# One hybrid encoder layer on one core: the mixers' due times paced by stage, the last block's cut moved from column 18 to 20, a stream of weight sums started later

## The chip, the cores and the metric

One core of a Trainium2 chip runs the whole program in one launch. The metric is device time in microseconds (us); three runs of the kernel before are at hand, and one profiled execution.

## The reference, cut to what matters

One layer over two streams of 1024-wide tokens: a prompt of 2048 behind 16 meta tokens, and 64 new sample tokens with their own states. A norm, one wide projection, three mixers that are causal scans over time, an output projection, and a SwiGLU block:

```python
def _trunk(x, states, segs, p):
    ...
        m, ns = _mixer(_rmsnorm(x, p['norm1_w'][l]), l, *st, segs, p)
        x = x + m
        x = x + _swiglu(_rmsnorm(x, p['norm2_w'][l]), p['w_gate'][l], p['w_up'][l], p['w_down'][l])
    ...
    return _rmsnorm(x, p['final_norm_w']), [jnp.stack(lst) for lst in new]

def _mixer(h, l, ssm0, conv0, rw0, shift0, hg0, segs, p):
    proj = jnp.einsum('btd,dn->btn', h, p['w_in'][l])
    z, xbc, dt_raw, rw_in, hg_in = _split(proj, [SSD_INNER, SSD_CONV_DIM, SSD_HEADS, RW_IN, HG_IN])
    ...   # y_ssd: chunked state-space scan; y_rw: RWKV-7 scan; y_hg: gated linear recurrence
    y = jnp.concatenate([y_ssd, y_rw, y_hg], axis=-1).astype(h.dtype)
    out = jnp.einsum('btm,md->btd', y, p['w_out'][l])

def _swiglu(h, wg, wu, wd):
    return (jax.nn.silu(h @ wg) * (h @ wu)) @ wd
```

Everything is float32. The hidden width of the SwiGLU block is 2816, which the kernel cuts into 22 columns of 128.

## The kernel before, in words

**Tokens and tiles.** The tokens stand in 17 tiles of 128 (tile 0 holds the 64 sample tokens and the 16 meta tokens). Each float32 product is done as three matmuls on parts `hi` and `lo`. A weight is split into its parts on first use (`load_unit`: a 256 KB load into the ring `raw`, ACT for `hi`, POOL or DVE for `lo`), stored to memory, and from the second use on loaded as a 512 KB pair into the ring `w` (5 buffers; `raw` has 3).

**Stages of the weight products.** The projection runs over three groups of tiles. Then come three early blocks of three tiles each (`EARLY`, class `Ffn`): `out` (the output projection, residual, norm, transposes), `ffn` (the 22 columns, two at a time, called a pair here: gate and up products, then `down` of the pair before), `rest` (the last down and the final norm). Block 0 uses the weights of `out` and `ffn` for the first time and so splits them; blocks 1 and 2 load the pairs. The eight last tiles (`LATE`) follow in another scheme (`tokens_first`, `columns`) that multiplies sums of weight quarters; `t_sums` forms these sums (loads into `raw`, four subtractions or additions on DVE, stores) and `prep_sums` does so for twelve of them ahead of time.

**The mixers** work beside the weight products, one tile after the other: stream `rw` (`rw_mixer`, `rw_tail`) and stream `hs` (`hg_mixer` and `ss_mixer` in step). Their small matmuls write the banks `c`, `h` and `po`, while the weight products write `g`. Much of a mixer is DVE and ACT work, and each goes through memory several times (`rin`, `hin`, `sin` loads; `psc` and `psx` of the small triangular solver). The outputs `y` are stored tile by tile and loaded again by `out`, for the late tiles into `ya`.

**The placing.** The order in which instructions are written comes from a clock in the code, `now`. Every weight product yields its cost in full-speed microseconds of TensorE (columns / 2360), and `flow` adds it to `now` and steps each stream that is due. A step yields its distance to the next one, and `Stream.step` sets the due time: `self.t = max(self.t, now[0] - 1.0) + d * self.scale`. The scales are 1.08 for rw, 1.03 for hs; an hs tile is 13 steps of 6.0. `drain` steps the streams until the outputs asked for are written, with no weight product between. This order is a priority: the framework builds each engine's queue from it by a simulated clock, and may set an instruction that is ready ahead of an earlier one that is not.

**Where the last block is cut.** `early()` writes block 2's columns up to `SWITCH` as a part of `flow`, then `drain(ALLY(range(NT)))` writes what is left of the mixers, their memory is given up, the 24 loads of `ya` and the remaining columns of block 2 follow. `prep_sums` is a stream like the mixers, appended after block 1's `out`.

Of the kernel before, what the change touches and what calls it, by code (L numbers as in the profile page):

```python
# [23 lines left out]
NFF = DFF // P  # L24
# [15 lines left out]
GLO = 3  # L40
URB = 6
RWX, HSX, HSD = 1.08, 1.03, 6.0
COL = 1 / 2360
AHEAD = 4
KOUT = [8, 9, 10, 11, 0, 1, 2, 3, 4, 5, 6, 7]
# [1 line left out]
DSTEP = (-1, 2, 6, 9)  # L47
FW = 3
NH = 4
SWITCH = 18  # L50
PRE = 3
TAIL = 4
CW = 384
# [25 lines left out]
def body(tc, A, O, blocks=None, supers=None, dbg=None):  # L79
# [7 lines left out]
    def pool(st, name, bufs=1, **kw):  # L87
        return st.enter_context(tc.tile_pool(name=name, bufs=bufs, **kw))
# [20 lines left out]
    def mm(out, lhsT, rhs, start, stop, more=False):  # L109

        return T.matmul(out, lhsT, rhs, start=start, stop=stop, skip_group_check=more)  # L111
# [145 lines left out]
    def gemm_cm(w, hTs):  # L257

        banks = [gbank() for _ in hTs]
        for k0 in range(0, KD, 4):  # L260
            hi, lo = load_unit(w[:, k0 * P:(k0 + 4) * P])
            for ps, ((hhi, hlo), n) in zip(banks, hTs):
                for k in range(k0, k0 + 4):
# [3 lines left out]
                    mm(ps[:, :n], wl, hhi[:, k, :n], False, k == KD - 1)  # L267
                yield 12 * n * COL
        return banks

    def gemm_tm(w, hT, tiles):

        banks = [gbank() for _ in tiles]
        for k in range(KD):
            wh, wl = load_unit(w[k * P:(k + 1) * P, :])
            for ps, (o, n) in zip(banks, tiles):
# [3 lines left out]
                mm(ps[:n], l, wh, False, k == KD - 1)  # L280
            yield 3 * len(tiles) * 512 * COL
        return banks

    def gemm_dt(w, hTs):
# [8 lines left out]
        for ps, ((hhi, hlo), n) in zip(banks, hTs):  # L293
            for k in range(KD):
                mm(ps[:16, :n], wt[:, k], hhi[:, k, :n], k == 0, False)
                mm(ps[:16, :n], wt[:, k], hlo[:, k, :n], False, k == KD - 1)
            yield 16 * n * COL
        return banks
# [686 lines left out]

    streams, done = [], set()
    ready = {"rw": [], "hs": []}
    now = [0.0]

    class Stream:  # L990
        def __init__(self, gen, scale):
# [2 lines left out]
        def step(self):  # L994
            d = next(self.gen, None)
            if d is None:
                self.live = False
            else:
                self.t = max(self.t, now[0] - 1.0) + d * self.scale

    def mixers(kind, fn):
        for t in range(last_tile + 1):
# [15 lines left out]
    def flow(gen):  # L1018

        for cost in gen:  # L1020
            now[0] += cost
            for s in list(streams):
                while s.live and s.t <= now[0]:
                    s.step()
            streams[:] = [s for s in streams if s.live]

    def drain(keys):
        while not all(k in done for k in keys):
            for s in list(streams):
                s.step()  # L1030
            streams[:] = [s for s in streams if s.live]
# [113 lines left out]
    class Ffn:  # L1145
# [31 lines left out]
        def out(self):  # L1177
# [10 lines left out]
            def scaled(i):  # L1188
                hs[i] = self.w2k(), self.w2k()
                rms_scaled(fp, acc[:, i, :], self.lens[i], nw, hs[i])  # L1190
# [5 lines left out]
            def mms(i, k, wh, wl):  # L1196
                yh, yl = (ya[0][:, k], ya[1][:, k]) if k < 8 else (y3[0][:, k - 8], y3[1][:, k - 8])
                ti = slice(i * P, i * P + P)
                mm(banks[i], yh[:, ti], wh, k == KOUT[0], False)
                mm(banks[i], yh[:, ti], wl, False, False)  # L1200
                mm(banks[i], yl[:, ti], wh, False, k == KOUT[-1])

            for half_ in range(2):
                cs = slice(half_ * 512, half_ * 512 + 512)
                banks = [gbank() for _ in tiles]
                for k in KOUT[:8] if half_ else KOUT:
                    w = load_unit(A["w_out"][half_, k])
                    for i in range(self.nt):
                        mms(i, k, *w)
                    yield 3 * self.nt * 512 * COL  # L1210
                if half_ == 0:
# [4 lines left out]
            for i in range(self.nt):  # L1216
# [3 lines left out]
                if i < 2:  # L1220
                    scaled(i)
                yield 12 * 512 * COL
            hi, lo = self.hT = self.hl(self.fp, "h2", KD)
# [25 lines left out]
        def rest(self):  # L1249
# [4 lines left out]
            for i in range(self.nt):  # L1254
                for hf in range(2):
                    self.down_tile(i, hf, mhi, mlo, wds[hf])
                    yield 3 * CF * 512 * COL
                self.final(i, fw)
# [25 lines left out]
    if supers:  # L1284
# [4 lines left out]
        def early():  # L1289
            drain(ALLY(EARLY[0]))  # L1290
            fs[0].start()
            for i, f in enumerate(fs):
                drain(ALLY(EARLY[i]))
                yield from f.out()
                if i == 1:
                    streams.append(Stream(prep_sums(), 1.0))
                if i + 1 < len(fs):
                    yield from f.ffn(0, NFF - AHEAD)
                    drain(ALLY(EARLY[i + 1]))
                    fs[i + 1].start()  # L1300
                    yield from f.ffn(NFF - AHEAD, NFF)
                    yield from f.rest()
                else:
                    yield from f.ffn(0, SWITCH)

# [9 lines left out]
        def t_sums(key, q, queue):  # L1315

            def ld(n):
                r = mk(ring, [P, 512], tag="raw", bufs=RB)
                queue.dma_start(r, q[n])
                return r  # L1320

            def st(n, r):
                d = tdram[key, n] = dram.tile([P, 512], F32, tag=f"{key}{n}", name=f"{key}{n}")
                G.dma_start(d, r)

            a, b = ld(3), ld(1)
            V.tensor_tensor(a, a, b, SUB)
            st("t3", a)
            c_ = ld(0)
            V.tensor_tensor(b, b, c_, SUB)  # L1330
            st("t1", b)
            V.tensor_tensor(c_, a, c_, ADD)
            st("t2", c_)
            d_ = ld(2)
            V.tensor_tensor(d_, d_, c_, SUB)
            st("t4", d_)

        def quarters(key, kk):
            if key in ("w_gate", "w_up"):
                return [A[key][2 * kk + f][:, h * 512:h * 512 + 512] for h in range(2) for f in range(2)]  # L1340
            if key == "wo":
                k = kk // 2 * 4 + kk % 2
                return [A["w_out"][d, k + 2 * h] for h in range(2) for d in range(2)]
            return [A["w_down"][(2 * kk + h) * P:(2 * kk + h + 1) * P, d * 512:d * 512 + 512] for h in range(2) for d in range(2)]

        def prep_sums():
            for key, kks in (("wo", (4, 5, 0, 1, 2, 3)), ("w_gate", range(PRE)), ("w_up", range(PRE))):
                for kk in kks:
                    t_sums(f"{key}{kk}", quarters(key, kk), nc.sync)
                    yield 35.0  # L1350

        def parts(raw):
            wt = mk(ring, [P, 2, 512], F32, tag="w", bufs=WB)
# [73 lines left out]
        xs2 = [[dram.tile([P, D], F32, tag=f"xs{h}{j}", name=f"xs{h}{j}") for j in range(NH)] for h in range(2)]  # L1427

        flow(early())
        drain(ALLY(range(NT)))  # L1430
        stA.close()
# [10 lines left out]
        lq = pool(st, "lq", side="right", reuse_waits="tile")  # L1442
        flow(fs[-1].ffn(SWITCH, NFF))
        flow(fs[-1].rest())
# [354 lines left out]
```

## Time and profile before

| | |
|---|---|
| three runs | 3514.22, 3523.47, 3526.61 us (median 3523.47) |
| profiled execution | 3511.97 us, span 3510.2 us |
| mean granted TensorE clock | 0.982 |
| busy: PE, PEld, DVE, ACT, POOL | 3366.0, 2942.8, 2212.6, 1226.9, 778.5 us |
| DMA | 860.42 MB, mean 245 GB/s |

The stages can be told apart in the timeline of TensorE by the tiles that its matmuls read:

| stage | from, to (us) |
|---|---|
| projection, with mixers | 0 to 1357 |
| block 0: out, columns | 1357 to 1476, to 1856 |
| block 1: out, columns | 1856 to 1950, to 2318 |
| block 2: out, columns | 2318 to 2397, to 2730 |
| late tiles | 2730 to 3510 |

How to read it: the span is that of one execution; engines overlap, and a stage's length is set by whichever wait ends last in it. PE and PEld are the two halves of TensorE (matmul and weight load). A clock of 1.00 is TensorE's full speed. DMA share is the busy share of the core's 16 DMA engines. In a table by stage, each engine's column is its busy time with the number of instructions in brackets.

### The profile page before, as it was taken

The numbers are of one execution on the slowest core, as the hardware profiler recorded it, in microseconds if no ns is written. First come the engines' busy times: TensorE is split into PE (matmuls) and PEld (weight loads), VectorE is DVE, ScalarE is ACT, GpSimd is POOL, SyncE is SP. The second block draws the span as 40 slices with busy tenths as digits, with TensorE's granted clock in tenths as the row PEclk, the third lists the DMA queues.
The fourth block names the chain that finished last, engine by engine and source line by source line (L and its number), as shares of the span: only waits on it lengthen the run. The fifth ranks groups of instructions, "written<-read, shape, count | busy, mean of one in ns | idle before, by whom it ended". The sixth has DMA issues, their size and how long they took to land.

```text
span 3510.2 us, 61013 instructions
## 1 busy us (share of the span) xinstructions
PE 3366.0 (96%) x22588; PEld 2942.8 (84%) x22588; DVE 2212.6 (63%) x4961; ACT 1226.9 (35%) x2635; POOL 778.5 (22%) x1122
## 2 busy tenths in 40 slices
PE   7999999999999998899898999999999999999998
PEld 7999789999799996787787888888988887888786
DVE  3358555567665677687877767667643676665453
ACT  4445233344343443343452212223210352233342
POOL 3324201102112112344442211111100123431101
PEclk9999999999999998899999999999999999999999
DMA  9776875565775667889889898686788567875856
GB/s 321 233 227 209 298 237 160 172 180 163 247 223 173 193 194 245 288 305 315 293 303 346 297 328 275 227 285 203 224 259 267 199 209 263 304 273 165 295 191 215
DMA packets 427123, 860.42 MB, mean 245 GB/s; under 512 B 112432, under 2 KB 212280, under 8 KB 424776
## 3 DMA queue, kind: packets, MB, share of 16 engines
q1 hardware_dynamic: 394376, 749.01, 64.9%
q0 software_dynamic: 32448, 107.50, 8.4%
q8 instruction: 178, 2.92, 0.3%
q14 instruction: 121, 0.99, 0.1%
HBM read 603.81 MB, written 252.54 MB: 244 GB/s over the span
## 4 chain that ended last, share of the span: by engine, by line
PE 69%; DMA 11%; DVE 10%; issue 4%; ACT 2%; POOL 2%; SPq 2%; POOLq 0%; DVEq 0%; ACTq 0%
PE g L111 47%; PE d L111 11%; PE c L111 5%; PE h L111 4%; DMA w<-w 3%; DMA raw<-in_w_up 1%; DMA hin<-hg 1%; POOL w L222 1%; DMA hg<-stage 1%; DVE tp L640 1%; DVE Xp L641 1%; DMA raw<-in_w_gate 1%; PE po L111 1%; DVE acc L1278 1%; DVE gcv L418 1%
## 5 line engine op out<-in xcount | busy, mean ns | idle before, releaser
L111 PE MATMUL g<-hhi,w 128*128 128x384 f32 (+3 forms) x3312 | 831.7, 330 | 10.1 <-POOL w L222 3.7
L111 PEld LDWEIGHTS g<-hhi,w 128*128 128x128 f32 (+1 forms) x3312 | 580.0, 188 | 23.9 <-POOL w L222 4.5
L111 PE MATMUL g<-h2hi,w 128*128 128x384 f32 (+1 forms) x2112 | 548.6, 335 | 21.9 <-DMA w<-w 7.9
L111 PE MATMUL g<-hlo,w 128*128 128x384 f32 (+3 forms) x1680 | 550.5, 328 | 0.0
L111 PEld LDWEIGHTS g<-h2hi,w 128*128 128x128 f32 x2112 | 376.4, 190 | 35.2 <-ACT w L220 8.6
L111 PE MATMUL g<-h2lo,w 128*128 128x384 f32 (+1 forms) x1056 | 349.6, 331 | 0.0
L111 PEld LDWEIGHTS g<-hlo,w 128*128 128x128 f32 (+1 forms) x1680 | 314.1, 187 | 6.2
L222 POOL TENSOR_TENSOR w<-raw,w 128x512 fp32r<-128x512 f32 x180 | 244.0, 1358 | 338.3 <-ACT w L220 276.3
L111 PE MATMUL g<-w,mhi 128*128 128x512 f32 x792 | 259.3, 404 | 8.3 <-DMA w<-w 3.5
L220 ACT ACTIVATE w<-raw 128x512 fp32r<-128x512 f32 x240 | 150.1, 628 | 194.2 <-PE g L111 50.0
L111 PEld LDWEIGHTS g<-h2lo,w 128*128 128x128 f32 x1056 | 200.3, 190 | 2.8
L111 PE MATMUL g<-w,hhi 128*128 128x512 f32 (+1 forms) x544 | 178.1, 407 | 7.4 <-DMA w<-w 4.2
L111 PEld LDWEIGHTS g<-w,mhi 128*128 128x128 f32 x792 | 145.0, 189 | 43.6 <-DVE acc L1278 4.5
L640 DVE TENSOR_TENSOR tp<-Xp,b4k 128x60 f32<-128x60 f32 (+24 forms) x527 | 125.1, 237 | 52.0 <-DMA b4k<-psc 38.9
L1278 DVE TENSOR_TENSOR acc<-g,acc 128x512 f32<-128x512 f32 (+1 forms) x198 | 132.1, 682 | 39.2 <-PE g L111 38.9
L111 PE MATMUL g<-w,mlo 128*128 128x512 f32 x396 | 155.7, 394 | 0.0
L111 PE MATMUL g<-w,op 128*128 128x512 f32 x600 | 142.8, 395 | 0.0
L111 PEld LDWEIGHTS g<-w,op 128*128 128x128 f32 x600 | 112.3, 187 | 27.3
L641 DVE TENSOR_TENSOR Xp<-Xp,tp 128x60 f32<-128x60 f32 (+24 forms) x527 | 122.9, 233 | 13.3
L230 POOL TENSOR_TENSOR rs<-ss,half 128x1 f32<-128x1 f32 (+2 forms) x51 | 34.6, 681 | 424.6 <-DVE ss L228 261.0
L111 PEld LDWEIGHTS g<-w,hhi 128*128 128x128 f32 (+1 forms) x544 | 99.5, 189 | 32.4 <-DMA w<-w 6.5
L356 DVE SCALAR_TENSOR_TENSOR stage<-graw,cvec,stage 128x384 f32<-128x384 f32 (+2 forms) x98 | 53.5, 549 | 113.5 <-ACT graw L351 34.4
(449 smaller groups left out, 6619.2 us busy)
## 6 DMA issues: line engine op xcount, KB each, us to landing
w<-w SPq DMA_DIRECT2D x893, 512.0 KB, 4.4
hin<-hg SPq DMA_DIRECT2D x16, 1280.0 KB, 7.7
rin<-rw SPq DMA_DIRECT2D x16, 896.0 KB, 6.2
raw<-in_w_gate SPq DMA_DIRECT2D x56, 256.0 KB, 4.4
raw<-in_w_up SPq DMA_DIRECT2D x56, 256.0 KB, 4.3
hg<-stage SPq DMA_DIRECT2D x64, 192.0 KB, 2.5
raw<-in_w_out SPq DMA_DIRECT2D x48, 256.0 KB, 4.4
sin<-ss SPq DMA_DIRECT2D x16, 768.0 KB, 4.9
```

What stands on the lines that cost most here:

```text
L111: return T.matmul(out, lhsT, rhs, start=start, stop=stop, skip_group_check=more)
L220: S.activation(hi, raw, AF.Copy)
L222: (G if units[0] % 4 < GLO else V).tensor_tensor(lo, raw, wt[:, 0], SUB)
L230: G.tensor_tensor(rs[:n], ss[:n], half[:n, 0:w], ALU.pow)
L356: V.scalar_tensor_tensor(st[:, a0:a1], raw[:, s0:s0 + a1 - a0], mu, st[:, a0:a1], MUL, ADD)
L418: V.scalar_tensor_tensor(cvt[:, :M], raw[:, j:j + M], tap(j), cvt[:, :M], MUL, ADD)
L640: V.tensor_tensor(tv, _bc(Xp[:, 0:m, q], 2, w), _bc(Up[:, q, q + 1:32], 1, m), MUL)
L641: V.tensor_tensor(Xp[:, 0:m, q + 1:32], Xp[:, 0:m, q + 1:32], tv, ADD)
L1278: V.tensor_tensor(self.acc[:n, i, cs], ps[:n], self.acc[:n, i, cs], ADD)
```

## The change

A factor `pace` multiplies the distance between the steps of every stream (mixers and sums alike). It is 1.0 through the projection, 1.36 from block 0's `out` on, 1.02 from block 1's on. Block 2 is cut at column 20 in place of 18. The stream of the sums is appended after ten columns of block 1 in place of none, and its steps are 32 apart in place of 35 (times the pace).

```diff
+PACE = (1.36, 1.02, 1.02)
...
-SWITCH = 18
+SWITCH = 20
+AFTER = 10
...
-    now = [0.0]
+    now, pace = [0.0], [1.0]
...
-                self.t = max(self.t, now[0] - 1.0) + d * self.scale
+                self.t = max(self.t, now[0] - 1.0) + d * self.scale * pace[0]
...
                 drain(ALLY(EARLY[i]))
+                pace[0] = PACE[i]
                 yield from f.out()
-                if i == 1:
-                    streams.append(Stream(prep_sums(), 1.0))
                 if i + 1 < len(fs):
-                    yield from f.ffn(0, NFF - AHEAD)
+                    if i == 1:
+                        yield from f.ffn(0, AFTER)
+                        streams.append(Stream(prep_sums(), 1.0))
+                    yield from f.ffn(AFTER if i == 1 else 0, NFF - AHEAD)
                     drain(ALLY(EARLY[i + 1]))
...
                     t_sums(f"{key}{kk}", quarters(key, kk), nc.sync)
-                    yield 35.0
+                    yield 32.0
```

## The prediction

> **What bounds the kernel now.** I read the page first (slices, then the matmul rows), then a table of busy time by stage with cuts at the borders of the stages, then the same table for the tile `g` alone (all weight products write a bank of that name), and last the waits of TensorE inside the stages that the change touches.
>
> ```profile
> span 3510.2 us, 61013 instructions
> PE   7999999999999998899898999999999999999998
> PEclk9999999999999998899999999999999999999999
> DMA  9776875565775667889889898686788567875856
> ```
>
> TensorE is busy in nearly every slice; the dull ones are 15 to 20, which is where the first early block runs. The stages in one table (out and feed-forward of block 0, of block 1, then block 2 in four pieces: out, columns with mixers beside them, columns without, the last 59 us):
>
> ```profile
> core 0: us, PE busy (x) PEld busy (x) DVE busy (x) ACT busy (x) POOL busy (x), PEclk, DMA share, GB/s
> 1357.00:1476.00 119.00, 96.09 (x655) 74.67 (x654) 86.86 (x186) 50.34 (x109) 36.96 (x33) 0.80 0.82 276
> 1476.00:1856.00 380.00, 352.55 (x2641) 306.01 (x2642) 297.14 (x610) 166.67 (x359) 166.30 (x133) 0.97 0.88 305
> 1856.00:1950.00 94.00, 81.15 (x586) 64.28 (x585) 64.84 (x176) 24.71 (x68) 21.13 (x31) 0.92 0.90 324
> 1950.00:2318.00 368.00, 361.58 (x2611) 323.45 (x2611) 261.53 (x633) 91.83 (x211) 56.50 (x71) 1.00 0.83 280
> 2318.00:2397.00 79.00, 73.84 (x629) 59.18 (x628) 49.21 (x138) 22.27 (x63) 12.41 (x19) 0.99 0.78 269
> 2397.00:2604.00 207.00, 206.77 (x1478) 189.87 (x1477) 121.03 (x301) 43.78 (x109) 23.29 (x23) 0.99 0.70 223
> 2604.00:2671.00 67.00, 57.40 (x285) 51.05 (x284) 27.34 (x36) 7.01 (x11) 0.00 (x0) 0.97 0.96 298
> 2671.00:2730.00 59.00, 59.00 (x306) 54.38 (x305) 20.47 (x34) 7.47 (x18) 0.82 (x2) 1.00 0.74 241
> ```
>
> Block 0 (1357 to 1856) leaves TensorE idle for 23 + 27 us, block 1 for 13 + 6, block 2 for 5 + 0 + 10 + 0. Block 0 is the only one that also splits weights (POOL 166 us in its columns against 57 in block 1's). The matmuls of `g` alone, and for the whole run those of the three banks that only mixers write:
>
> ```profile
> 1357.00:1476.00 119.00, 63.30 (x243) 44.45 (x242) 8.49 (x16) 4.54 (x10) 0.80 0.82 276
> 1476.00:1856.00 380.00, 284.25 (x1477) 233.83 (x1478) 63.63 (x110) 9.47 (x22) 0.97 0.88 305
> 1950.00:2318.00 368.00, 301.97 (x1478) 257.85 (x1479) 68.55 (x111) 11.42 (x23) 1.00 0.83 280
> 2397.00:2604.00 207.00, 176.77 (x885) 155.06 (x886) 38.73 (x62) 6.84 (x14) 0.99 0.70 223
> ...
> 0.00:3511.00 3511.00, 300.78 (x4556) 233.64 (x4556) 264.00 (x471) 201.64 (x455) 41.61 (x77) 0.98 0.74 245
> ...
> 0.00:3511.00 3511.00, 274.77 (x2792) 221.92 (x2792) 173.68 (x359) 26.79 (x51) 0.98 0.74 245
> ...
> 0.00:3511.00 3511.00, 35.66 (x816) 34.00 (x816) 10.11 (x17) 0.98 0.74 245
> ```
>
> The last three rows give the size of a mixer tile: (4556 + 2792 + 816) / 17 = 480 matmuls for one tile of both streams. All matmuls of a stage less those of `g` are mixers: 1164, or 2.42 tiles, in block 0's columns; 1133, 2.36 tiles, in block 1's; 593, 1.24 tiles, in block 2's; 412, 0.86 tiles, in block 0's out.
>
> **What a tile costs where it stands now.** The products have their cost in the code, in units of the placing clock: a block's out is 49.9 units, block 0's columns 229.2 (320 tokens), block 1's 257.7 (384 tokens), a pair of columns 15.6 and its down products 7.8. The last 59 us hold two pairs and three downs, 54.7 units, and no mixer: 1.08 us a unit. By that, block 0's columns would take 247 us alone, so 133 us went with 2.42 tiles: 55 us a tile. Block 1: 368 − 278 = 90 for 2.36, 38 a tile. Block 2, 2397 to 2604: the 885 products are about seven pairs and six downs less a little, 155.5 units or 168 us, so 39 for 1.24, 32 a tile. The same work costs 55 us beside block 0 and 32 us beside block 2. That difference is what the change can collect.
>
> **Pace of block 0: 1.36.** No instruction is added or removed; due times move, and with them the order on every queue (TensorE, DVE, ACT, POOL, and SP with `rin`, `hin`, `sin`, the solver's `psc`/`psx` trips). I followed the placing rule of `flow` and `Stream.step` through the yields with both sets of constants. At the end of block 0 the hs stream stands at tile 10.83 before and 10.00 after, the rw stream at 12.51 and 11.81. So 0.83 hs tiles and 0.70 rw tiles leave block 0: 0.77 tiles, 0.14 of them from its out, 0.63 from its columns. At the block's own price the columns give back 0.63 × 55 = 35 us. The out stage is mostly a hand-over, so I price its share at block 1's 38: 5 us. Sum −40.
>
> What is late next in block 0:
>
> ```profile
> PE g L111 <- ACT w L220: 8.0, 5, 3.3
> PE h L111 <- ACT us L920: 4.4, 2, 2.3
> PE g L111 <- POOL w L222: 3.6, 7, 0.9
> PE g L111 <- DVE w L222: 2.5, 4, 1.0
> ```
>
> These are TensorE's longest waits in 1476 to 1856. The products' own waits (rows of `g`) are for split weights, 14 us, and the rest for mixer steps that came due too soon. Fewer mixers shorten the second kind, not surely the first: a weight takes 256 KB in and 512 KB out whatever stands beside it. DMA had 0.88 × 380 = 334 us of work there. A mixer tile brings at least two large loads:
>
> ```profile
> hin<-hg SPq DMA_DIRECT2D x16, 1280.0 KB, 7.7
> rin<-rw SPq DMA_DIRECT2D x16, 896.0 KB, 6.2
> ```
>
> 2.2 MB, at 305 GB/s 7 us, so 4.5 us for 0.63 tiles. The fullest stretch in the table is 0.96, and (334 − 4.5) / 0.96 = 343 us: the columns can shrink by 37 us before DMA is the floor, and my 35 lies just inside. For that reason I take nothing for the 1.8 tiles that stay in block 0 becoming cheaper (they could: 1.8 × (55 − 38) = 30, of which the floor lets 2 through).
>
> **Pace of blocks 1 and 2: 1.02, and SWITCH 18 to 20.** Columns 18 and 19 and one more down join the stretch with mixers, 23.4 units. In block 1 the count of mixers stays (3.62 hs tiles before, 3.68 after). In block 2 the last hs step was due in pair 6 of the columns, 59 units ahead of the final drain; after, it comes due with the last down before the drain, and one step is left to it. So 0.77 tiles go beside pairs 7 to 9, at the price of block 2: 0.77 × 32 = +24. Bounds: 29 at block 1's price, and 14 if they fill the 9.6 idle us of 2604 to 2671. That idle time I leave in, because its cause moves along:
>
> ```profile
> PE g L111 <- DMA w<-w: 8.9, 6, 2.4
> ...
> 2602.13 0.55 POOL L883 DMA_DIRECT2D y<-hin  x1 [3.99 <-DVE hin L882]
> ...
> L1441 SPq DMA_DIRECT2D ya<-y x24: 518/630/1752, 2605.1 to 2633.4; - x24
> ```
>
> The 24 loads of `ya` start 3 us after the last mixer output and fill DMA (0.96) for some 30 us, and TensorE waits for weights meanwhile. After the change they start at the end of pair 9's downs, with pair 10 and two downs to run: 31 units, 34 us, and 43 with the same waits. The next stage needs the first third of `ya` at its start and the last third 11 us later, so 30 us fit, with little left. I take 0 here; the other bound is a lag of the chain as long as 20 us.
>
> **Sums later** (after column 10 of block 1, 32 apart in place of 35).
>
> ```profile
> L1319 SPq DMA_DIRECT2D raw<-in_w_out x24: 328/333/792, 1846.1 to 1998.2; - x24
> ...
> L1319 SPq DMA_DIRECT2D raw<-in_w_up x12: 328/333/1117, 2066.1 to 2123.6; - x12
> ```
>
> By the placing clock they were due from the start of block 1's columns (1950) to block 2's third down. They ran from 1846 to 2124, as soon as block 0's last weight had left the `raw` ring: independent work is pulled ahead of its place. I expect that again, so the later place moves them little: 0. If they do move, out 1 is rid of them, where TensorE waited for loaded weights in this row (1856 to 1950), and that is the bound below:
>
> ```profile
> PE g L111 <- DMA w<-w: 6.5, 4, 3.6
> ```
>
> Against it 5 us at most, were the 12 sums (48 DVE subtractions and 25 MB) to run beside `ya` instead.
>
> **Sum.** −35 − 5 + 24 + 0 + 0 = −16 us. The profiled execution took 3511.97 us (span 3510.2), 11.5 below the median of the runs, 3523.47. So 3496 for an execution like the profiled one, and 3507.5 as a median. A difference of 0.3%, 10.6 us, is about what a measurement of this kernel can tell from no change.
>
> **Rivals.**
> 1. Block 0 is held by its weights, and the mixers only fill the holes. Then its columns don't shrink by 55 a tile but by little more than block 2 charges. For it: 14 us of waits for split weights and DMA at 0.88. Against it: TensorE was busy 352 of 380 us and DMA has room up to 0.96. With 38 a tile: −24 − 5 + 24 = −5; with 32, 0; with a floor some us higher, +5: 3518 to 3528. Chance 0.28.
> 2. The end of block 2 turns into a wait, and the kernel gets slower. Place: the border to the last tokens at 2730. The last mixer output lands late, `ya` behind it, and the weights of pair 10 interleave with 6 MB on a full DMA. It decides from a lag of about 16 us beyond the 34 to 43 us of cover. For it: both streams have round trips through memory, and no step of theirs is left to trail behind in slack. Against it: TensorE waited 0.2 us for mixers between 2397 and 2604, so they keep up there. Worth +8 to +25: 3531 to 3549. Chance 0.16.
> 3. The hand-over from out to columns in block 0 closes, since fewer mixer steps stand on DVE ahead of the norm. That stage took 119 us against 79 in block 2, with DVE at 87 and 49 us busy. Half of that difference would bring 20 us more: 3479 to 3497. Against it: the stage's first 25 us are a wait for the previous stage's buffers, where the pace isn't set yet. Chance 0.08.
> The granted clock goes with the third: 0.80 in that stage, 0.99 in the same stage of block 2. The Trainium skill, TensorE: Matmul & The Clock Gate, section "Part 1: The HAM clock gate", has it that about 3.4 us without matmul work halves the clock until a busy window has passed; the trace agrees in that 0.80 goes with 23 idle us of 119. By that rule 119 × 0.2 = 24 us are the most that steady work could win back there, an estimate, and it would put the time at the third rival's.
> That the sums stay where they ran is my own forecast; it changes no case.
>
> **How the numbers follow.** My forecast, −5 to −25 around −16, 3498 to 3518: 0.48. Rival 1: 0.28, rival 2: 0.16, rival 3: 0.08. Faster by over 0.3% (below 3513): three quarters of the forecast, 0.36, rival 3, 0.08, and a small part of rival 1 where the columns do shrink, 0.06: 0.50. Slower (above 3534): 0.15 from rival 2 and 0.02 from a high rival 1: 0.17. Same: 0.33. The likeliest case alone spans 3498 to 3518. The range goes from rival 3's middle, 3487, to the lower part of rival 2, 3533; outside stay half of rival 3 and most of rival 2, under 0.2.
>
> **What would show it.** Right: block 0's columns near 345 us in place of 380, with about 860 mixer matmuls in them in place of 1164; block 1's columns within 8 us of 368; 2604 to 2671 filled with mixers, the last `y<-hin` some 25 to 35 us before the last columns' end; the raw loads of the sums still starting near block 0's end. Wrong: DMA at 0.93 or more in block 0 with `g` waiting for split weights over 25 us (rival 1); a wait of the first products after block 2 for `ya` or `op` (rival 2); block 0's out under 105 us (rival 3). The forecast falls if the price of a mixer tile beside block 0 doesn't come from its density there.

## The result, and the profile after

The changed kernel took 3563.91 us (median of 4 runs, 3559.21 to 3567.03) against 3522.72 for the kernel before on the same chip: a ratio of 1.0116, interval 1.0099 to 1.0133. That is 41 us slower. The prediction had 3507.5, with a chance of 0.17 for slower; its range ended at 3533.

The page after, its span and TensorE's row of slices:

```profile
span 3562.8 us, 60980 instructions
...
PE   7999999999999998899888999999998999999998
```

TensorE has a new dull slice, the 31st (2672 to 2761): the end of block 2. The stages with cuts at the borders of this execution: out and columns of block 0, of block 1, then block 2 as out, columns up to the last pair, and the last pair to the border.

```profile
core 0: us, PE busy (x) PEld busy (x) DVE busy (x) ACT busy (x) POOL busy (x), PEclk, DMA share, GB/s
1359.70:1476.50 116.80, 94.05 (x646) 73.45 (x645) 83.71 (x184) 49.28 (x106) 36.51 (x32) 0.81 0.80 278
1476.50:1864.90 388.40, 357.39 (x2615) 303.32 (x2614) 285.28 (x604) 158.90 (x345) 169.41 (x129) 0.97 0.87 302
1864.90:1953.70 88.80, 77.61 (x447) 61.88 (x443) 62.91 (x146) 30.12 (x76) 20.23 (x31) 0.94 0.92 322
1953.70:2304.40 350.70, 342.29 (x2310) 306.29 (x2310) 222.33 (x543) 71.27 (x162) 43.53 (x60) 0.99 0.82 278
2304.40:2401.80 97.40, 84.80 (x659) 66.21 (x658) 51.09 (x118) 28.31 (x74) 15.55 (x22) 0.92 0.66 233
2401.80:2721.20 319.40, 315.42 (x2331) 285.49 (x2329) 190.12 (x483) 63.11 (x153) 29.08 (x30) 0.99 0.70 222
2721.20:2778.10 56.90, 37.37 (x183) 33.39 (x183) 24.37 (x33) 11.34 (x29) 2.96 (x4) 0.82 0.84 249
```

Block 0's columns are 388 us, not 345. They still hold 2615 matmuls, and the rows of `g` alone have 1468 of them, so 1147 are mixers where the prediction had 860. Block 1's columns, where it expected no change, are 17 us shorter; out 2 is 18 us longer; block 2's columns (the last two rows) are 44 us longer.

The stages of both kernels, with the mixer matmuls m that start in each (counted record by record). In columns 0 this gives 1188 and 1162, where differences of rows give 1164 and 1147: a view of the tile `g` also holds eight matmuls of each rw tile that read a tile of that name.

| | out 0 | columns 0 | out 1 | columns 1 | out 2 | columns 2 | rest of the span |
|---|---|---|---|---|---|---|---|
| before, us | 118.4 | 379.9 | 94.3 | 367.6 | 79.7 | 331.9 | 2138.3 |
| before, m | 412 | 1188 | 346 | 1156 | 390 | 606 | |
| change, us | −1.7 | +8.5 | −5.5 | −16.9 | +17.6 | +44.4 | +6.1 |
| change, m | −8 | −26 | −144 | −298 | +26 | +450 | |

The sum is +52.6. The medians differ by 41: the profiled execution of before was 11.5 us below its median. The projection, where the change does nothing, took between 1352 and 1367 us in the profiled executions; columns 0 took 378.9 to 384.3 us in five of them that hold the same 1188 mixer matmuls (before, e2, e3, e11, e12). So differences of a few us in one stage are not read. The table says it in one line: one tile (476 matmuls) left blocks 0 and 1, mostly block 1, for 16 us, and came to block 2 for 62.

**Where the tiles went.** The outputs of the hs stream in time, after and then before (start, duration, instruction, and in brackets POOL's idle time before it):

```profile
1723.83 0.62 POOL L885 DMA_DIRECT2D y<-hin  x1 [1.45 <-DVE hin L884]
1812.95 0.59 POOL L885 DMA_DIRECT2D y<-hin  x1 [0.74 <-DVE hin L884]
1935.71 0.59 POOL L885 DMA_DIRECT2D y<-hin  x1 [8.90 <-DVE Xp L643]
2234.80 0.62 POOL L885 DMA_DIRECT2D y<-hin  x1 [10.42 <-DVE hin L884]
...
2731.95 0.55 POOL L885 DMA_DIRECT2D y<-hin  x1 [3.82 <-DVE hin L884]
```

```profile
1719.90 0.61 POOL L883 DMA_DIRECT2D y<-hin  x1 [1.25 <-DVE Xp L641]
1848.44 0.61 POOL L883 DMA_DIRECT2D y<-hin  x1 [3.84 <-DVE hin L882]
1933.33 0.54 POOL L883 DMA_DIRECT2D y<-hin  x1 [4.07 <-DVE hin L882]
2130.15 0.54 POOL L883 DMA_DIRECT2D y<-hin  x1 [1.13 <-DVE hin L882]
```

The stream that was to be held back by 36% wrote its eleventh tile at 1812.95, 35 us earlier than before. By its due times that tile was to begin only at the start of out 1. One tile later comes a gap of 299 us (1935.71 to 2234.80), where before had an output at 2130, and the last output moves from 2602 to 2732. The rw stream did slow down: its twelfth output moves from 1802.68 to 1875.88. A tile of rw has 316 matmuls, one of hs 164. In the first ten pairs of block 0's columns hs rose from 2.20 to 2.71 tiles and rw fell from 2.18 to 1.36, 176 matmuls fewer in all; those ten pairs took 331.4 us before and 332.3 after. The last pair, with the two downs behind it, took 150 of them back: 240 rw matmuls ran there in place of 44, and it is 7.7 us longer (before, then after):

```profile
1807.30:1855.80 48.50, 44.70 (x308) 37.04 (x306) 43.40 (x64) 29.97 (x70) 18.31 (x15) 1.00 0.84 291
```

```profile
1808.70:1864.90 56.20, 51.13 (x457) 40.76 (x456) 39.66 (x84) 22.34 (x49) 23.09 (x18) 0.94 0.92 325
```

In the whole of columns 0 rw falls from 734 to 670 matmuls and hs rises from 454 to 492.

**The end.** TensorE's waits in the last 57 us of block 2, and the loads behind them:

```profile
PE g L113 <- DVE ya L1471: 19.5, 1, 19.5
```

```profile
L1445 SPq DMA_DIRECT2D ya<-y x24: 594/832/1039, 2736.9 to 2756.3; - x24
```

One single wait of 19.5 us, from 2743.5 to 2763.1. The row names DVE's work on `ya`, but the matmul that waits is `g<-w,mhi`, a down product of block 2, which reads a weight and no `ya`. SP's queue shows what it waits for:

```profile
2715.53 18.00 SPq L218 DMA_DIRECT2D w<-w  x8
2736.87 20.18 SPq L1445 DMA_DIRECT2D ya<-y  x24
2757.45 2.36 SPq L218 DMA_DIRECT2D w<-w  x5
```

The next weight was issued only behind the 24 loads, at 2757.45, and a load took some 5 us to land there. In e1, e3, e6 and e14 below, SP's queue has the same order, and in all but e3 the wait is put down to `DMA w<-w`. The first of the 24 loads waited for the store of the last output:

```profile
SPq L1445 <- DMA y<-hin: 3.2, 1, 3.2
```

It reads another tile; in the kernel `ya` takes memory that the mixers give up, so this is a wait for memory (read from the code, not tested). In the kernel before, seven weight loads stood between the 24, which took from 2605 to 2635, and TensorE lost 9.6 us. The last output is now 46 us before the border, not 128.

### The profile page after: what moved, and what is told of

The parts are those of the page before. It is cut to its first block, busy times and chain, and to the rows that moved or that the text cites. A ratio compares the mean times of both kernels' runs of the same rounds, so it can differ in the third digit from the quotient of the medians.

```text
span 3562.8 us, 60980 instructions
## 1 busy us (share of the span) xinstructions
PE 3390.1 (95%) x22588; PEld 2952.6 (83%) x22588; DVE 2202.9 (62%) x4961; ACT 1226.7 (34%) x2635; POOL 776.5 (22%) x1122
## 4 chain that ended last, share of the span: by engine, by line
PE 62%; DMA 13%; DVE 12%; issue 6%; ACT 2%; POOL 2%; SPq 2%; DVEq 0%; POOLq 0%; ACTq 0%
PE g L113 44%; PE d L113 7%; PE c L113 5%; PE h L113 4%; DMA w<-w 3%; DMA raw<-in_w_down 2%; DVE tp L642 1%; DVE Xp L643 1%; DMA hg<-stage 1%; DMA hin<-hg 1%; DMA raw<-in_w_gate 1%; DVE acc L1280 1%; PE po L113 1%; DMA x<-in_x_prompt 1%; DMA raw<-in_w_up 1%
## 5 line engine op out<-in xcount | busy, mean ns | idle before, releaser
L113 PE MATMUL g<-w,mhi 128*128 128x512 f32 x792 | 266.9, 411 | 28.9 <-DVE ya L1471 19.5
L113 PE MATMUL d<-ya,w 128*128 128x512 f32 x528 | 124.6, 392 | 1.8 <-DMA w<-w 1.8
```

## The experiments

Ratios are to runs of the kernel before on the same chip; stage lengths are from each run's one profile.

**Parts of the change.** Pace of block 0 alone, with the two columns more:

```
PACE = (1.36, 1.0, 1.0)   SWITCH = 20   AFTER = 0   sums 35.0 apart
```

> The pace of block 0 alone: 1.36, 1.0, 1.0, the cut at column 20, the sums at their old place. Theory A (the pace does not take the hs mixer out of block 0, because the framework's ordering sets it ahead of its due time there; it only pushes the later due times back, so mixers leave block 1 and land at block 2's end, where the loads of ya come too late): nearly the whole loss, +30 to +42 us, ratio 1.008 to 1.012; hs outputs of tiles 9 to 11 as early as before, the last one near 2720, a wait for ya of 10 to 20 us. Rival B (the sums or the 1.02 cost the time): within 10 us of before. Rival C (many small shifts): about half the loss, +20.

Measured: 3550.8, 1.0086 [1.0071, 1.0101]. Columns 0 +8.8, columns 1 −18.2, out 2 +14.4, columns 2 +38.6 us, with the changed kernel's counts within 8 in every stage. The whole pattern comes from this one number; it is worth about 30 of the 41 us. The end waits here too, with the 24 loads of `ya` issued from 2716 to 2738:

```profile
PE g L113 <- DMA w<-w: 18.5, 1, 18.5
```

The rest without that pace:

```
PACE = (1.0, 1.02, 1.02)   SWITCH = 20   AFTER = 10   sums 32.0 apart
```

> The change without the pace of block 0: 1.0, 1.02, 1.02, the cut at column 20, the sums later. Theory A: within 10 us of before (0.997 to 1.003), last hs output near 2612 in place of 2602, the sums' loads from 1846 to about 2130 as before. Rival B (sums or 1.02): the loss is here, +25 us or more.

Measured: 3531.86, 1.0031 [1.0019, 1.0044]. In no stage does the mixer count change by more than 6, and there is no wait at the end. Some 11 us come from it; 30 and 11 make the 41, each known to some 5 us. Which of the two parts, the pace or the sums, two more runs tell:

```
PACE = (1.0, 1.0, 1.0)    SWITCH = 18   AFTER = 10   sums 32.0 apart
```

> The sums alone: after column 10 of block 1, 32 apart, pace 1.0 everywhere, the cut at 18. The change without the first pace (E2) lost 9 us, and this or the 1.02 did it. Theory: the loads of the sums still run from about 1846 to 2130 and the mixers stand where they stood: within 5 us of before. Rival: the sums' DVE work moves behind the mixers of block 1 and block 2 and costs +6 to +12.

```
PACE = (1.0, 1.02, 1.02)  SWITCH = 20   AFTER = 0    sums 35.0 apart
```

> Pace 1.0, 1.02, 1.02 with the cut at 20 and the sums at their old place. Last hs output 9 units later than before. Theory: +2 to +8, since 0.02 of the later tiles moves to the end of block 2 at 32 us a tile and the ya loads with them. Rival: 0, and E2's 9 us were the sums.

Measured: the sums alone 3520.11, 1.0003 [0.9992, 1.0014]; the 1.02 with the switch 3529.74, 1.0026 [1.0011, 1.0041]. The raw loads of the sums ran from 1844 to 2119 with the change of their place, and from 1846 to 2124 without it: their place does nothing. So the 11 us (9 in this run) belong to the 1.02 and the switch, which were not tried apart. The counts hardly move; the profile has +5.8 in columns 1 and +10.8 in columns 2, too little in one execution to name a wait.

**Is it the late end?** Block 0 and 1 as before, the last block stretched:

```
PACE = (1.0, 1.0, 1.4)    SWITCH = 20   AFTER = 0   sums 35.0 apart
```

> The late end by itself: pace 1.0, 1.0, 1.4, sums at their old place, cut at 20. Blocks 0 and 1 keep the order of before, the last hs output goes to about 2715. Theory A: the wait for ya at the border (19.5 us after the change) comes back at 12 to 20 us, the weights' wait of 9 us beside the ya loads goes, so +5 to +12 us in all. Rival: the end is what costs, +30 or more. Rival: no wait since the loads fit beside pair 10, 0.

Measured: 3529.68, 1.0021 [1.0009, 1.0033]. The wait is there in full,

```profile
PE g L113 <- DVE ya L1471: 18.8, 1, 18.8
```

but columns 2 grew by only 9.9 us and the total by 7: before had its own idle time behind the `ya` loads (9.6 us at 2604 to 2671), and that went. So the end is worth 7 to 10 of the 41 us, not 20. The opposite test lets block 1 take back what block 0 gives, so that the end is early again:

```
PACE = (1.36, 0.6, 1.0)   SWITCH = 20   AFTER = 0   sums 35.0 apart
```

> Pace 1.36 in block 0, 0.6 in block 1, 1.0 in block 2, sums at their old place, cut at 20: block 0 as after the change, the hole in block 1 filled, the last hs output well before 2600. Theory A: the loss is gone, within 10 us of before (0.997 to 1.003), with no wait for ya. Rival D (block 0's own 5 to 9 us and out 2's 18 us come from block 0's pace itself): +15 to +30 stay.

Measured: 3552.7, 1.0095 [1.0079, 1.0112]. There is no wait at the end, and it is as slow as e1. My theory at that time, that the gap in block 1 and the crowd at the end were the whole loss, fell here. Columns 0 were +15.5 with 1164 mixer matmuls, columns 2 +10.8 and out 2 +7.2, and no other stage gained; why is open.

**Which stream?** The pace for one stream alone:

```
-   self.t = max(self.t, now[0] - 1.0) + d * self.scale
+   self.t = max(self.t, now[0] - 1.0) + d * self.scale * (pace[0] if self.scale == RWX else 1.0)
    PACE = (1.36, 1.0, 1.0)   SWITCH = 20        # the second run: == HSX
```

> Pace 1.36 in block 0 for the rw stream alone; hs, blocks 1 and 2, the sums as before, the cut at 20. Catch-up (E4) kept the loss without the late end, so theory A in its first form has fallen. Theory B: the hand-over stage out of a block has holes in which mixers cost nothing; what leaves it lands beside dense columns at about 35 us a tile. Here out 1 loses half its mixers, block 2's columns gain about 0.5 tile, the last hs output stays near 2600 (no wait for ya): +15 to +25 us, block 0's columns +5 to +9 with as many mixers as before. Rival D' (it is the hs stream's bursts that cost block 0): 0 to +6.

> Pace 1.36 in block 0 for the hs stream alone, the rest as before, the cut at 20. In this order the hs stream does slow down in block 0 (tile 11 leaves it). Theory B: block 0's columns lose about 0.2 tile and gain nothing or little (0 to -8), out 1 loses mixers, block 2 ends late with the wait for ya (about 19 us, less the 9 us of weights' waits): +15 to +28 in all. Rival (my prediction's price: 55 us a tile saved in block 0): block 0's columns under 365, total within 8 us of before.

Measured: rw alone 3542.72, 1.0078 [1.0061, 1.0095]; hs alone 3528.04, 1.0025 [1.0012, 1.0039]. With rw alone, columns 0 keep 1170 mixer matmuls and the first ten pairs take 331.5 us, with 2.77 hs and 1.37 rw tiles. That is the changed kernel's block 0, with no pace on hs at all: in columns 0 rw loses 62 matmuls and hs gains 44, and the 10.9 us by which they grow lie in the last pair, with 240 rw matmuls. (The profiled execution of e5 is 9 us below its median.) With hs alone, 78 matmuls leave columns 0, 38 of hs and 40 of rw; the columns give 8.7 us, and out 1 gives 7.6; a wait of 17.8 us at the end and 272 more matmuls in columns 2 take them back. So a pace on rw opens room, which hs fills whether its due times are late (after) or not (e5); with no pace on rw, hs does fall back, by about a quarter of a tile.

A stronger and a quicker pace say the same:

```
PACE = (2.5, 1.0, 1.0)    # e7, else as e1
PACE = (0.8, 1.0, 1.0)    # e8, else as e1
```

> Pace 2.5 in block 0 (both streams), 1.0 after it, sums as before, cut at 20. If due times bound the streams in block 0, its mixers would fall to a good half and its columns well below 350 us. Theory B: the hs stream still runs ahead of its due times there (tiles 8 to 11 as early as after the change), block 0's columns stay within 15 us of 380, and the mixers are missing in block 1's columns and crowd block 2: over 70 us slower than before, most of it in block 2's columns.

> The other direction: pace 0.8 in block 0, 1.0 after it, sums as before, cut at 20. More mixers in block 0's columns (about 0.2 tile), fewer in block 2's, the last hs output near 2530. Theory B: out 1 and out 2 keep nearly their mixers, block 0's waits take a part of the extra ones for free: -8 to +4 us. Rival (the prediction's price): block 0's columns grow by 55 us a tile, +5 to +12.

Measured: e7 3563.93 against 3520.07, a single run without an interval, with 2.73 hs and 1.24 rw tiles in the first ten pairs and 332.7 us there: 2.5 does to them what 1.36 does. e8 3537.26, 1.0055 [1.004, 1.007]: 76 more matmuls in columns 0 went with 8.0 us more, columns 1 took 15.6 us more with 28 more matmuls, and columns 2 gave only 5.0 for 120 fewer. Both runs miss the totals that I expected: e7 is 44 us slower in place of over 70, e8 slower than either of its two cases. Neither direction of this pace pays.

**The price of a tile.** Mixers left out, the rest as before:

```
 hs_mixer(t):  # e9: tiles 8 to 15; e10: tile 9 alone
-    the mixer
+    load hin and sin, store y from them, 13 yields without work
```

> What a tile of the hs stream costs in each stage. The kernel before, without the hs mixers of tiles 8 to 15: their loads and stores of y stay (the stores write the loaded rows), the steps in between do nothing. In the trace of before 2.8 of these tiles ran beside block 0's columns, 2.5 beside block 1's, 1.7 beside block 2's. The prediction's price (55, 38, 32 us for a tile of both streams, a bit under half of it hs): block 0's columns -65 to -75 us, block 1's -40 to -45, block 2's -22 to -27, hand-overs little. Theory C (the split weights hold block 0's columns, mixers fill the holes): block 0's columns fall by less a tile than block 1's, -20 to -40 us in all; the out stages fall by under 10 us each.

> The kernel before without the hs mixers of tile 9 alone (its loads and stores of y stay), a tile whose due time lies in block 0's columns. The prediction's price: block 0's columns -20 to -25 us. Theory B (the order fills block 0's holes again with the next tiles; what is missing is missing where TensorE is full): block 0's columns within 8 us of before with as many mixers, block 1's columns -10 to -18 us with about 0.3 tile less in them, -12 to -25 us in all.

Measured: e9 3451.31 (two runs), 0.9804 [0.9773, 0.9835]. Out 1 gave 16.7 us, columns 1 40.0 for 2.35 hs tiles and 74 rw matmuls, columns 2 24.3 for 1.7. But columns 0 grew by 16.2 us with 316 fewer matmuls, where I had expected them to shrink. The empty steps of later tiles ran together at 1533 to 1583, with DMA full in that stretch (the 1.00),

```profile
1533.00:1583.00 50.00, 39.23 (x189) 33.70 (x187) 28.54 (x83) 14.24 (x25) 18.23 (x17) 0.86 1.00 346
```

so this is no clean price of block 0. e10 3520.99, 1.0003 [0.999, 1.0016]: a tile's hs matmuls left out in block 0, and columns 0 hold 1186 as before. The next tiles moved up, and block 1's columns had 184 fewer and took 9.9 us less; but columns 0 took 9.8 us more with the same count, and the 12 to 25 us that I expected in all did not come. The room in block 0 is filled even when the work that was in it doesn't exist.

**Holding hs in place.** These runs make hs stay behind: in block 0 no hs matmul or transpose may be put ahead of the weight products written before it.

```
+        if pin[0] == "hs" and pinning[0]:            # pinning[0] = (i == 0)
+            order this matmul after the last one written outside both streams
 PACE = (1.0, 1.0, 1.0) e13; (1.36, 1.0, 1.0) e14; (1.36, 0.85, 0.9) e15; (2.5, 1.0, 1.0) e16
 SWITCH = 20   AFTER = 0   sums 35.0 apart
```

> The kernel before (paces 1.0, sums as before, switch at 20), with one order added: while block 0 runs, a matmul or transpose of the hs stream may not be put ahead of the weight products that were written before it. It is the ground for the next run. In the order built, block 0's columns hold 627 units of mixer matmuls against 642 before, out 1 161 against 218, block 1's columns 668 against 606, the last hs step comes at the same place. Prices that I found so far (27 us a tile beside block 1, about 34 beside block 2, a hole of out 1 lost for nothing) give +0 to +15: 3520 to 3535. If holding the hs matmuls makes TensorE wait for their steps, +20 or more, and then the next run is read against this one alone.

> The same order as the run before, with the pace 1.36 in block 0. Now the hs stream cannot move ahead into the room that the rw stream leaves: in the order built, block 0's columns lose 116 units of mixer matmuls (some 215 matmuls, 0.45 tile), and block 2's columns gain 154 (0.6 tile). Against the run before: the prediction's price (55 us a tile beside block 0) gives block 0's columns -25, block 2's +19, and the total -6 before any wait for the last tile. If the columns of block 0 are held by their split weights and the mixers fill holes, they give back 0 to -8, and the total is +11 to +25. A wait for ya at the end of up to 20 us comes on top in both, since the last hs step comes 75 units later.

> The same order, with paces 1.36, 0.85 and 0.9: what leaves block 0 is put beside block 1, and the last hs step comes 57 units earlier than in the run before. By the prediction's price (55 beside block 0, 38 beside block 1) it is the best of all: -25 in block 0's columns, +17 in block 1's, 0 at the end, and 3512 to 3520 against 3520 before. If block 0's columns do not give the price back, it is +10 to +25 above the held ground run, as e4_catch_up was above before.

> The held order of e13 and e14, with the pace of block 0 at 2.5. In the order built, block 0's columns keep 461 units of mixer matmuls (627 in e13, 511 in e14), so some 310 matmuls or 0.65 tile less than e13. If e14 said the right thing (the columns are held by their split weights and by the order around them), they stay at 375 to 383 us, TensorE waits longer for split weights than e14's 25.6 us, and the rows of POOL and ACT as releasers grow. If instead mixers cost their 55 us a tile there and e14 was an accident of one order, the columns come to 345 us. The total is of no interest (the mixers pile up beside block 2).

Measured: e13 3528.09, 1.0017 [1.0003, 1.0031]; e14 3550.45, 1.0076 [1.0057, 1.0096]; e15 3556.31, 1.0084 [1.0064, 1.0104]; e16 3573.38 against 3520.59, a single run. Now tiles leave block 0. Its columns in e13, e14 and e16, all matmuls and then `g` alone:

```profile
1467.00:1847.60 380.60, 346.97 (x2609) 305.22 (x2607) 301.21 (x617) 166.45 (x356) 164.75 (x130) 0.95 0.88 305
1467.00:1847.60 380.60, 286.93 (x1477) 240.08 (x1477) 65.47 (x111) 9.93 (x23) 0.95 0.88 305
```

```profile
1478.10:1857.10 379.00, 343.03 (x2392) 291.54 (x2391) 257.00 (x520) 147.63 (x306) 159.25 (x122) 0.96 0.86 298
1478.10:1857.10 379.00, 293.81 (x1469) 238.21 (x1469) 63.52 (x109) 9.52 (x22) 0.96 0.86 298
```

```profile
1479.90:1834.30 354.40, 328.45 (x2318) 280.11 (x2317) 232.62 (x478) 142.76 (x294) 148.60 (x117) 0.99 0.89 314
1479.90:1834.30 354.40, 281.03 (x1469) 231.40 (x1469) 64.78 (x111) 9.55 (x22) 0.99 0.89 314
```

From e13 to e14, 216 mixer matmuls (1154 to 938, 0.45 tile) leave and the columns give 1.6 us; to e16, 290 leave (864, 0.60 tile) and they give 26.2. In e14 TensorE waits for split weights instead:

```profile
PE g L114 <- POOL w L243: 11.3, 16, 2.0
PE g L114 <- ACT w L241: 8.4, 7, 3.5
PE g L114 <- DVE w L243: 5.9, 6, 2.3
```

That is 25.6 us (18.8 in e13, 14 before); in e16 it is 18.4, and the same rows of `g` (1469 matmuls) take 13 us less. So e14 alone would have shown rival 1 (block 0 is held by its weights), and e16 takes half of it back: there is no floor at 380. I expected 375 to 383 for e16, and that fell. The price is neither 55 a tile nor nothing. Part of it is which matmuls leave: by the prediction's three rows of banks, busy time over count, an rw matmul keeps TensorE busy for 63 ns and an hs one for 98, 36 us for a tile of both. By this estimate e6 takes 6 us of TensorE's work out of columns 0, e14 19 and e16 28, and the columns gave 8.7, 1.6 and 26.2. Two of the three fit; why e14 does not, beyond its longer waits for weights, is open.

On the other side the moved work was paid for. From e13 to e14, columns 2 take 268 matmuls more and 28 us, 20 of them in the last pair, where

```profile
PE g L114 <- DMA w<-w: 17.9, 1, 17.9
```

stands in e14 and nothing in e13. From e13 to e16, 791 matmuls (1.65 tiles) leave the stages from out 0 to out 2, which get shorter by 50 us, 30 a tile; they come to columns 2, which get longer by 82. e15 brings the last output early enough that no wait there is longer than 3.3 us, and its profile is still 28 us above that of e13: 9 in out 1, 5 in columns 1, 11 in columns 2 and small pieces. Even with the tiles held in place, no pace of block 0 paid.

**What holds the split weights?** In block 0's columns of the kernel before, SP's queue waits like this to store weights that POOL has not finished, with loads behind:

```profile
SPq L224 <- POOL w L222: 127.3, 74, 5.7
```

So the stores went to POOL's queue:

```
-        nc.sync.dma_start(d, wt)
+        nc.gpsimd.dma_start(d, wt)
```

> The kernel before, in which the stores of the split weights go out through POOL's queue behind POOL's subtraction, not through SP's. In SP's queue those stores waited 127 us for POOL in block 0's columns, with the loads of the next raw weights and the mixers' loads behind them. If SP's order is what holds the weights in block 0, TensorE's 14 us of waits for split weights there fall by half or more, and the total is -5 to -20. If the holder is the split itself (the raw load, then ACT, then POOL in their order), nothing changes there, or POOL's issue of 512 KB stores makes it worse: 0 to +20.

Measured: 3534.73, 1.005 [1.0029, 1.007]. The waits for split weights did not halve,

```profile
PE g L112 <- ACT w L221: 7.8, 7, 3.4
...
PE g L112 <- DVE w L223: 5.2, 2, 4.6
```

13 us, and 1.0 for POOL, against 14, and columns 0 grew by 15.6 us with 42 more matmuls. So SP's order is not what holds them.

No version here that does all the work beats the kernel before; the sums alone equal it.

## Why the prediction was wrong

**The step that failed: "So 0.83 hs tiles and 0.70 rw tiles leave block 0".** I followed the due times through the yields, and treated them as places. Where the streams stood at the end of block 0, in tiles (the trace's figures are estimates, read between the times of two outputs):

| | by due times: before, after | in the trace: before, after |
|---|---|---|
| hs | 10.83, 10.00 | 11.1, 11.4 |
| rw | 12.51, 11.81 | 12.3, 11.9 |

rw fell back by about half of what I had, and hs went ahead in place of back. Counted in matmuls, out 0 and columns 0 together lost 72 of rw and gained 38 of hs, 0.23 tile of each. Instead of 0.63 tiles, 26 matmuls of 480 left the columns, and the term −35 measured +8.5. I had the rule in the same text: "independent work is pulled ahead of its place" was my reason for leaving the sums at 0. It holds for the mixers as well. e5 (rw alone) and e10 (the tile left out) show the refill; e14 and e16 show that tiles do leave when hs is held. What the 7.7 us more of the last pair pay for, beside 150 more matmuls, was not tested.

**The price behind it, 55 us a tile, was an average that I used as a margin.** Where matmuls did leave, e6 gave 8.7 us for 78 (54 a tile, but hardly more than one execution differs from another), e14 1.6 for 216 (4), e16 26.2 for 290 (43). Rival 1's mechanism, waits for split weights over 25 us, showed in e14 alone, and in the changed kernel not at all: 16.5 us in these rows.

```profile
PE g L113 <- ACT w L222: 8.5, 6, 2.1
PE g L113 <- POOL w L224: 5.7, 10, 1.2
PE h L113 <- ACT us L922: 5.4, 2, 3.1
PE h L113 <- DVE hin L834: 2.5, 3, 1.3
PE g L113 <- DVE w L224: 2.3, 3, 1.4
```

**Out 0, −5:** −1.7, with 8 matmuls fewer. **Block 1 "within 8 us":** it lost 442 matmuls in out 1 and columns for 22 us, 244 of rw and 198 of hs. This is the other half of the failed step. In e5, where hs has no pace, the 44 hs matmuls that came into block 0 are the 44 that block 1 lacks. In the changed kernel hs lacks far more than the 38 that it took ahead: the due times of both streams lie later from block 0 on and don't move up (`max(self.t, now - 1)`), and what that leaves empty is block 1, not block 0. In out 1, 144 matmuls left for 5.5 us, 18 a tile.

**Block 2, +24:** +44.4. Its first ten pairs took 319.3 us with 1044 mixer matmuls. e3 has the late end with the matmuls of before, 606, and took 287.4: 438 matmuls, 0.91 tile, went with 32 us, 35 a tile. So the price of 32 was about right, and the number of tiles was too small. The wait at the end made most of what is left. **The wait for `ya`, taken as 0 with 20 as the other bound:** 19.5, by a mechanism near that of rival 2 (a late last output, loads behind it), but of a product inside block 2 for a weight, not of the first products behind it for `ya`. Rival 2 had the weights interleave with the 24 loads; they stood behind them all. e3 sizes it by itself: 18.8 us of wait, 7 of total, since 9.6 us of older idle time go. So rival 2 was right in kind, and too small alone to make the 41 us.

**Out 2, +17.6, was in no term.** It holds 26 more matmuls than before and 12.6 idle us in place of 5, with the clock at 0.92 in place of 0.99. Its waits after:

```profile
PE h L113 <- DVE us L941: 3.6, 1, 3.6
PE g L254 <- DVE w2k L248: 3.0, 2, 1.9
PE g L113 <- DMA w<-w: 2.3, 1, 2.3
PE h L113 <- DVE dec L977: 1.7, 1, 1.7
```

hs and ss steps stand in TensorE's queue ahead of the transposes of the stage, and DVE serves both. This is read from the trace and was not tested by itself. The idle time makes 7.4 of the 17.6 us, and the clock some 7 by an estimate from half of 15.5 us: it was 0.50 for 10.2 us near the start of the stage and for 5.3 at its end.

```profile
2304.40:2311.20 6.80, 3.52 (x20) 2.60 (x18) 5.13 (x13) 0.85 (x4) 3.66 (x7) 1.00 0.64 165
2311.20:2321.40 10.20, 9.46 (x82) 7.19 (x83) 3.08 (x6) 0.38 (x1) 2.20 (x4) 0.50 0.98 381
```

The Trainium skill, TensorE: Matmul & The Clock Gate, section "Part 1: The HAM clock gate", has a gap of some 3.4 us lower the clock. For the 5.3 us the trace agrees, they begin as the wait of 3.6 us ends; for the 10.2 us it does not: the longest wait before them is 2.3 us, in a stretch where TensorE was busy for 3.52 of 6.8 us. The measurement decides: here several shorter waits did it too. So it was in block 0's out before, which the prediction put to that rule: the clock was 0.50 there from 1361.6 to 1385.5, and no wait of the stage was longer than 2.8 us.

**Right:** the sums at 0 (e11, 1.0003), and about block 2's price. The idle time of 2604 to 2671 did not move along: it went, and the one long wait came in its place. **Still open:** where the 11 us of the 1.02 and the switch come from, with unchanged counts; why e4, without the late end, keeps the loss; and why a tile beside block 0 gives 4 to 43 us when it leaves.

## What to carry to other kernels

A due time or a priority in a program that a scheduler reorders is not a place: before pricing a move, look in the trace of before for work that ran ahead of its due time (the sums did, 100 us ahead), and expect any other ready stream to fill the room that you open. What it takes ahead is missing later, and what was pushed back crowds the end. When a view names what ended a wait, look at what the waiting instruction reads: the wait at the end was put down to `ya` and was for a weight behind `ya` in the queue. Read a price per tile from two states of the same stage, not from the stage's average: here the average was 55 us, and removing work gave 4 in one run and 43 in another.

## What the runs showed of the hardware

The clock fell to 0.50 for 10.2 us behind a stretch of 6.8 us in which TensorE was busy for 3.5, with no wait longer than 2.3 us (out 2 after the change). How much that costs a stage can't be read from its mean clock alone: the 1469 matmuls of `g` in block 0's columns took 281.0 us at 0.99 (e16) and 293.8 at 0.96 (e14), with 26 and 36 idle us around them, but 1477 took 286.9 at 0.95 with 34 idle us (e13).

The stores of the split weights are not free on POOL: in e17's row of that stage

```profile
1463.70:1859.30 395.60, 357.79 (x2685) 311.40 (x2683) 314.68 (x617) 166.22 (x357) 232.38 (x258) 0.94 0.84 297
```

POOL is busy for 232 us with 258 instructions, against 166 with 133 before; 125 more of them cost 66 us, 0.5 each. On SP the issue of a load took 0.6 to 1.0 us at the end of block 2, and 24 in a row held the queue for 20.2 us, with the weights behind them. DMA was full meanwhile (a share of 1.06 from 2736.9 to 2757.0), so the issue and the transfer can't be told apart as what set that length.
